# A layer-norm and weight-split step taken off GpSimd: one two-scalar VectorE operation for a chunk, all weight splits on VectorE

## The chip, the cores and the metric

The kernel runs on one core of a Trainium2 chip. The metric is the device time of one execution in microseconds (us). The engines are TensorE (PE), VectorE (DVE), ScalarE (ACT), GpSimd (POOL) and SyncE (SP), which only issues transfers here. Two times count as different when they are over 0.2% apart.

## The reference

Two layers of a block on 256 tokens of width 2048. Each layer projects its input, runs three mixers on the parts (a gated convolution, a gated linear recurrence, a retention), projects back, adds and normalizes, then does a feed-forward step of width 8192 and normalizes again. What touches the change is this:

```python
def layer_norm(x, g, b):
    xf = x.astype(jnp.float32)
    mu = jnp.mean(xf, axis=-1, keepdims=True)
    var = jnp.mean(jnp.square(xf - mu), axis=-1, keepdims=True)
    return (xf - mu) * lax.rsqrt(var + LN_EPS) * g + b

def reference(...):
...
    for l in range(DEPTH):
        proj = jnp.einsum('btd,de->bte', x, w_in[l])
...
        h = jnp.einsum('bte,ed->btd', mix, w_out[l])
        x = layer_norm(DEEPNORM_ALPHA * x + h, ln1_g[l], ln1_b[l]).astype(dtype)
        f = jnp.square(jax.nn.relu(jnp.einsum('btd,df->btf', x, w_ff1[l])))
        h = jnp.einsum('btf,fd->btd', f, w_ff2[l])
        x = layer_norm(DEEPNORM_ALPHA * x + h, ln2_g[l], ln2_b[l]).astype(dtype)
    return x
```

There are four such norms: two per layer.

## The kernel before, in words

**Weights in two parts.** All large products run as float32r matmuls of split numbers: a value is its rounded high part plus a low part. Weights come from memory in pieces of 1 MB into one of three `raw` buffers (`load2`, L268). A piece is two *units* of 128 x 1024. For each unit `unit()` lets ACT write the high part (L288) and then another engine the low part, raw minus high (L291), into one of six `wp` buffers. DVE does L291, except where `pool_lo` names the unit: there POOL does it.

**Products with the activation standing still.** `xstat` makes an output block of 512 columns for both halves of the tokens (`t` = 0 and 1, 128 tokens each) from eight units. `mmx` issues six matmuls (L313) per unit and half: for each of two row blocks high x high, high activation x low weight, low activation x high weight. With `tail` = 6 the last six units run all of t = 0 first, then all of t = 1, so that the norm of the first half can start early. With `head` = 6 the next product starts with units 1 to 6 of t = 0 before t = 1 comes in.

**The norm.** The class `Norm` runs at the end of such a product. For each half, the last of four chunks of 512 columns is added (L938 or L940), its statistics taken (L861), mean and variance combined (L872), epsilon added (L873). POOL raises the variance to the power -1/2 (L407), which gives the reciprocal deviation, and then multiplies mean and reciprocal, negated (L413, `nb`). DVE meanwhile takes chunks 0 to 2 minus mean times gain (L883), then times reciprocal plus bias (L889). Chunk 3 is *lazy*: its gain and bias are applied behind the transposition, so it needs only (x - mean) x reciprocal, which ACT does as scale and bias (L893) with the reciprocal and `nb`. PE transposes each chunk (L399, four 128 x 128 blocks); for chunk 3 ACT applies gain and bias (L913, four instructions); then ACT casts the high part (L388) and DVE makes the low part (L390), and the matmuls of the next product can use it. In the last norm of the kernel all four chunks go by L883 and L889 and then to memory, and `nb` is not read.

**The order.** Nothing is ordered by hand: `Plan.run` lists all operations with an engine, a cost, what they read and write, and picks for each engine, in simulated time, what can start earliest, by urgency. The order on each engine is then fixed, and the engines wait for each other by semaphores. An operation waits for its engine's earlier ones in any case. The norm's operations are given the highest urgency (`FIRST`, `NOW`), the low parts of weights are due when their matmuls are.

**Names.** `wp_64` to `wp_69` are the six `wp` buffers; at the first norm they hold units 1 to 6 of the next product. `act_72` to `act_75` hold the transposed activations that the norm makes, `act_76` to `act_79` the old ones, `aux_105` to `aux_108` the transposes in PSUM, `mm_101` to `mm_104` the sums. At the first norm `mm_102` is the last sum of t = 1 before the norm, `mm_103` the next product's for t = 0 and `mm_104` for t = 1. `sm_98` and `sm_99` hold the statistics of the two halves.

Of the kernel before, what the change touches and what calls it, by code (L numbers as in the profile page):

```python
# [14 lines left out]
AF = mybir.ActivationFunctionType  # L15
ALU = mybir.AluOpType
# [6 lines left out]
W = 512  # L23
# [17 lines left out]
WARM = 11  # L41
HEAD, TAIL = 6, 6

POOL_LO = (1, 3)


PACK = (("ident", P), ("tri", P), ("lbt", 12), ("hng", 12), ("rgg", 12), ("rgb", 12), ("clg", 8), ("clb", 8),
# [25 lines left out]
class Plan:  # L73
# [8 lines left out]
    def op(self, eng, cost, fn, r=(), w=(), slack=8.0, floor=8.0, need=None, after=(), chain=None, late=0.0, same=None):  # L82
        o = Op()
        o.eng, o.cost, o.fn, o.slack, o.floor, o.need, o.late = eng, cost, fn, slack, floor, need, late
        o.same = (0.0 if eng == "PE" else self.SAME) if same is None else same
        o.succ, o.ready, o.main, o.end = [], 0.0, None, None
        deps = {}
        bufs = []
        for items, wr in ((r, False), (w, True)):
            for it in items:  # L90
                b, part = it if isinstance(it, tuple) else (it, None)
                if b not in bufs:
                    bufs.append(b)
                keep = []
                for (p, pp, pw) in b.log:
                    hit = pp is None or part is None or pp == part
                    if hit and (wr or pw) and p is not o:
                        deps[p] = True
                        if wr and (part is None or pp == part):
                            continue  # L100
                    keep.append((p, pp, pw))
                keep.append((o, part, wr))
                b.log = keep
        for p in after:
            if p is not None:
                deps.setdefault(p, True)
        if chain is not None:
            p = self.last.get(chain)
            if p is not None:
                deps.setdefault(p, False)  # L110
            self.last[chain] = o
        for b in bufs:
            if b.ring is not None:
                b.uses += 1
        o.bufs = bufs
        o.deps = deps
        o.left = len(deps)
        for p, full in deps.items():
            p.succ.append((o, full))
        self.ops.append(o)  # L120
        return o
# [81 lines left out]
def block_kernel(ctx: ExitStack, tc: tile.TileContext, a: dict, out: bass.AP):  # L203
    nc = tc.nc
    V, S, G = nc.vector, nc.scalar, nc.gpsimd
# [3 lines left out]
    op = plan.op  # L209
# [14 lines left out]
    def keep(name, shape, dt=F32):  # L224
        return Buf(None, pool.tile(list(shape), dt, name=name))


    def act(n, ptr=0, ps=False):
        return 0.000833 * n + (0.051 if ps else 0.093) + 0.093 * ptr

    def dve(n, ptr=0, fast=False):
        return (0.00052 if fast else 0.001042) * n + 0.069 + 0.06 * ptr

    POOLC, POW = 0.26, 1.5
# [159 lines left out]
    def transpose4(src, r, **kw):  # L394
        pt = aux.buf()

        def fn():
            for i in range(4):
                nc.tensor.transpose(out=pt.t[:, i * P:(i + 1) * P], in_=src()[:, i * P:(i + 1) * P], identity=ident)  # L399

        op("PE", 0.44, fn, r=r, w=[pt], **kw)
        return pt

    def rsqrt(v, s, c0, n):

        y = s[:, c0:c0 + n]
        G.tensor_tensor(out=y, in0=v, in1=mhalf.t[:, 0:n], op=ALU.pow)  # L407
        return y

    def rsqrt1(s, mean, v):  # L410

        y = rsqrt(v, s, 37, 1)
        G.tensor_scalar(out=s[:, 48:49], in0=mean, scalar1=y, scalar2=-1.0, op0=ALU.mult, op1=ALU.mult)  # L413

    NOW, FIRST = dict(slack=-50.0, floor=-100.0), dict(slack=-200.0, floor=-300.0)

    mhalf = keep("mhalf", [P, 4])
# [416 lines left out]
    class Norm:  # L834
# [31 lines left out]
        def norm(self, t):  # L866
            if self.xT is None and not self.last:
                self.xT = [acts.buf() for _ in range(4)]
            s = self.s[t]
            mean, rstd, nb = (lambda: s.t[:, 24:25]), (lambda: s.t[:, 37:38]), (lambda: s.t[:, 48:49])  # L870
            def aggr():
                V.bn_aggr(out=s.t[:, 24:26], in_=s.t[:, 0:24])  # L872
                V.tensor_scalar(out=s.t[:, 26:27], in0=s.t[:, 25:26], scalar1=EPS, scalar2=None, op0=ALU.add)  # L873

            op("DVE", 0.2, aggr, w=[s], **FIRST)

            def rs():
                rsqrt1(s.t, mean(), s.t[:, 26:27])

            op("POOL", POW + POOLC, rs, r=[(s, "x"), mhalf], w=[(s, "r")], **FIRST)  # L880
            direct = range(4) if self.last else [c for c in range(4) if c not in LAZY]
            for c in direct:
                op("DVE", dve(W, 1), lambda c=c: V.scalar_tensor_tensor(  # L883
                    out=self.y(t, c), in0=self.y(t, c), scalar=mean(), in1=self.gb[c][0].t, op0=ALU.subtract,
                    op1=ALU.mult), r=[(s, "x"), self.gb[c][0]], w=[(x_nat, (t, c))], **NOW)
            for c in range(4):
                xk = (x_nat, (t, c))
                if c in direct:
                    op("DVE", dve(W, 1), lambda c=c: V.scalar_tensor_tensor(  # L889
                        out=self.y(t, c), in0=self.y(t, c), scalar=rstd(), in1=self.gb[c][1].t, op0=ALU.mult,  # L890
                        op1=ALU.add), r=[(s, "r"), self.gb[c][1]], w=[xk], **NOW)
                else:
                    op("ACT", act(W, 2), lambda c=c: S.activation(  # L893
                        out=self.y(t, c), in_=self.y(t, c), func=AF.Identity, scale=rstd(), bias=nb()),
                       r=[(s, "r")], w=[xk], **NOW)
                if self.last:
                    op("DMA", 0.8, lambda c=c: nc.sync.dma_start(
                        out=out[t * P:(t + 1) * P, c * W:(c + 1) * W], in_=self.y(t, c)), r=[xk], **NOW)
                    continue
                cols = slice(t * P, (t + 1) * P)  # L900
                if c not in LAZY:
                    if c not in direct:
                        self.affine(c, t, **NOW)
                    pt = transpose4(lambda c=c: self.y(t, c), [xk, cst], **NOW)
                    split_act(self.xT[c], slice(0, 4), cols, lambda pt=pt: pt.t, [pt], t, ps=True, **NOW)
                else:
                    pt = transpose4(lambda c=c: self.y(t, c), [xk, cst], **NOW)
                    z = r2.buf()

                    def fn(c=c, pt=pt, z=z):  # L910
                        for b in range(4):
                            k = 4 * c + b
                            S.activation(out=z.t[:, b * P:(b + 1) * P], in_=pt.t[:, b * P:(b + 1) * P],  # L913
                                         func=AF.Identity, scale=lng[:, self.n, k:k + 1], bias=lnb[:, self.n, k:k + 1])

                    op("ACT", 4 * act(P, 2, True), fn, r=[pt, cst], w=[z], **NOW)
                    split_act(self.xT[c], slice(0, 4), cols, lambda z=z: z.t, [z], t, **NOW)
# [28 lines left out]
    for l in range(DEPTH):  # L946
# [3 lines left out]
        def vgroup(g, **kw):  # L950
            tl = []
            vt.append(tl)

            def done(t, ps):
                v = r2.buf()
                op("ACT", act(W, ps=True), lambda: S.copy(out=v.t, in_=ps.t), r=[ps], w=[v], floor=1.5)
                tl.append(v)

            xstat(a["wv"][l, g], xT, done, **kw)
# [9 lines left out]
        else:  # L969
            vgroup(0, head=HEAD, pool_lo=POOL_LO)  # L970
            norm.rest()
        pairs, gates = {}, {}
        for i, (kind, p) in enumerate(ORDER):
# [11 lines left out]
            if l == 0 and i == 1:  # L985
                op("DMA", 6.0, lambda: nc.sync.dma_start(out=x_nat.t, in_=a["x"].rearrange("(t p) d -> p t d", p=P)),
                   w=[x_nat], after=(plan.last["PE"],))
            if kind == "hf":
                hgrn_gates(l, p, pr, pair)
            elif kind == "hq":  # L990
                Qv = pv(pair, 2)
                op("ACT", act(W), lambda Qv=Qv, pr=pr: S.activation(out=Qv(), in_=pr.t, func=AF.Sigmoid), r=[pr],
                   w=[(pair, "Q")])
                op("DVE", dve(W), lambda Qv=Qv, pr=pr: V.tensor_tensor(out=Qv(), in0=pr.t, in1=Qv(), op=ALU.mult),
                   r=[pr], w=[(pair, "Q")])
            elif kind == "hg":
                gate = r2.buf()
                op("ACT", act(W), lambda gate=gate, pr=pr: S.activation(out=gate.t, in_=pr.t, func=AF.Sigmoid),
                   r=[pr], w=[gate])
                hgrn(l, p, pairs["h", p], gate, vt, mixT)  # L1000
            elif kind in ("cg", "ca"):
# [4 lines left out]
                if kind == "cg":  # L1006
                    op("ACT", act(W), lambda uv=uv, pr=pr: S.activation(out=uv(), in_=bl(pr.t, 2), func=AF.Sigmoid),
                       r=[pr], w=uk)
                else:
                    op("DVE", dve(W), lambda uv=uv, pr=pr: V.tensor_tensor(out=uv(), in0=bl(pr.t, 2), in1=uv(),  # L1010
                                                                           op=ALU.mult), r=[pr], w=uk)
# [5 lines left out]
            elif kind == "rg":  # L1017
                gate = r2.buf()
                op("ACT", act(W), lambda gate=gate, pr=pr: S.activation(out=gate.t, in_=pr.t, func=AF.Sigmoid),
                   r=[pr], w=[gate])  # L1020
                op("DVE", dve(W), lambda gate=gate, pr=pr: V.tensor_tensor(out=gate.t, in0=pr.t, in1=gate.t,
                                                                           op=ALU.mult), r=[pr], w=[gate])
# [10 lines left out]
        for c in range(NCH):  # L1033
# [9 lines left out]
            if c == 0:  # L1043
                xstat(a["w1x"][l], xT, square_t, head=HEAD, pool_lo=POOL_LO)
                norm.rest()
            for q in range(2 if c == 0 else 0, 8):
                r = wstat(a["w1"][l, 8 * c + q - 2], xT)
                f = r2.buf()
                op("DVE", dve(W), lambda f=f, r=r: V.scalar_tensor_tensor(  # L1049
                    out=f.t, in0=r.t, scalar=0.0, in1=r.t, op0=ALU.max, op1=ALU.mult), r=[r], w=[f], floor=1.5)  # L1050
# [127 lines left out]
```

## Time and profile before

| what | value |
|---|---|
| median of 3 runs | 2340.0 us (2339.7 to 2341.8) |
| the profiled execution, its own time | 2341.02 us |
| its span, first to last instruction | 2339.2 us |
| mean granted TensorE clock | 0.998 |
| PE, DVE, ACT, POOL busy | 2320.4, 1504.0, 1054.0, 65.0 us |
| first norm's PE stretch, from the first transpose of t = 0 to the first matmul of t = 1 | 447.18 to 464.16 us |

The span is the profile's, from the first instruction to the last; the execution's own time is 1.8 us longer. PE's busy time is that of matmuls, which overlap; a wait of PE is read from the timeline, where the idle time ahead of an operation stands in brackets with what ended it. Lines are those of the kernel before.

### The profile page before, as it was taken

How to read it: one execution, taken by the hardware profiler on the slowest of the kernel's cores; microseconds unless marked ns; L12 is line 12 of the kernel's file. 1: busy time of each engine (PE TensorE's matmuls, PEld its weight loads, DVE VectorE, ACT ScalarE, POOL GpSimd, SP SyncE). 2: the span in 40 equal slices, each digit the busy share in tenths (PEclk: the TensorE clock that was granted, in tenths of full speed). 3: DMA queues.
4: the chain of work that ended last, by engine and by line, in shares of the span. 5: the costliest groups of instructions: out<-in, count | busy, mean ns of one | idle time of the engine just before them, and what ended most of it. 6: DMA issues, size and time to landing. Idle time of an engine off the chain costs nothing.

```text
span 2339.2 us, 29616 instructions
## 1 busy us (share of the span) xinstructions
PE 2320.4 (99%) x12067; PEld 1974.0 (84%) x12067; DVE 1504.0 (64%) x2046; ACT 1054.0 (45%) x1334; POOL 65.0 (3%) x66
## 2 busy tenths in 40 slices
PE   9999999999999999999999999999999999999998
PEld 7888888788888888888888888887888888888886
DVE  6997666665565565565579976656655655655655
ACT  6445444454344344344444455444543444443442
POOL 0000000100000000000000000101000000000000
PEclk9999999999999999999999999999999999999999
DMA  8544566465555555556454445564555555555563
GB/s 299 181 162 162 171 198 207 162 207 188 190 189 189 198 180 198 188 190 205 167 205 162 163 162 174 189 218 159 205 198 185 193 187 191 185 193 198 181 229 113
DMA packets 67705, 439.90 MB, mean 188 GB/s; under 512 B 7664, under 2 KB 7920, under 8 KB 16624
## 3 DMA queue, kind: packets, MB, share of 16 engines
q1 hardware_dynamic: 67568, 438.01, 55.0%
q8 instruction: 94, 1.54, 0.2%
q14 instruction: 43, 0.35, 0.0%
HBM read 432.74 MB, written 2.10 MB: 186 GB/s over the span
## 4 chain that ended last, share of the span: by engine, by line
PE 98%; DVE 1%; DMA 0%; ACT 0%; issue 0%; SPq 0%; DVEq 0%
PE mm L313 44%; PE mm L363 33%; PE mm L365 17%; PE aux L604 2%; PE aux L399 1%; DVE x_nat L889 0%; DMA raw<-in_wv 0%; PE aux L550 0%; PE aux L552 0%; PE aux L588 0%; PE aux L548 0%; PE aux L717 0%; DVE x_nat L883 0%; ACT r L913 0%; DVE sm L861 0%
## 5 line engine op out<-in xcount | busy, mean ns | idle before, releaser
L291 DVE TENSOR_TENSOR wp<-raw,wp 128x1024 fp32r<-128x1024 f32 (+1 forms) x796 | 970.9, 1221 | 602.4 <-ACT wp L288 600.6
L288 ACT CAST wp<-raw 128x1024 fp32r<-128x1024 f32 (+1 forms) x802 | 842.4, 1052 | 819.0 <-PE mm L313 561.7
L363 PE MATMUL mm<-act,wp 128*128 128x512 f32 x3328 | 1180.8, 399 | 0.0
L313 PE MATMUL mm<-wp,act 128*128 128x512 f32 x4608 | 1061.1, 390 | 3.9 <-ACT wp L288 1.7
L313 PEld LDWEIGHTS mm<-wp,act 128*128 128x128 f32 x4608 | 861.1, 188 | 185.4 <-ACT wp L288 2.9
L365 PE MATMUL mm<-act,wp 128*128 128x256 f32 x3328 | 933.2, 280 | 0.0
L363 PEld LDWEIGHTS mm<-act,wp 128*128 128x128 f32 x3328 | 625.4, 188 | 151.5
L365 PEld LDWEIGHTS mm<-act,wp 128*128 128x128 f32 x3328 | 628.4, 189 | 0.5
L372 ACT COPY r<-mm 128x256 f32<-128x256 f32 x208 | 77.9, 375 | 369.6 <-PE mm L365 369.3
L375 DVE TENSOR_TENSOR r<-mm,r 128x256 f32<-128x256 f32 x184 | 78.1, 424 | 146.2 <-ACT r L372 145.9
L791 DVE SCALAR_TENSOR_TENSOR r<-u_t,cst,r 128x256 f32<-128x256 f32 x240 | 102.1, 479 | 0.0
L407 POOL TENSOR_TENSOR sm<-sm,mhalf 128x4 f32<-128x4 f32 (+1 forms) x24 | 30.4, 1266 | 2252.5 <-DVE sm L873 1589.4
L388 ACT CAST act<-r 128x512 fp32r<-128x512 f32 x82 | 51.5, 628 | 21.7 <-DVE r L1049 16.2
L390 DVE TENSOR_TENSOR act<-r,act 128x512 fp32r<-128x512 f32 x82 | 57.9, 706 | 0.0
L604 PEld LDWEIGHTS aux<-pair 128*128 128x128 f32 x336 | 42.4, 191 | 2.6
L1049 DVE SCALAR_TENSOR_TENSOR r<-r 128x512 f32<-128x512 f32 x60 | 41.6, 693 | 2.1
L604 PE MATMUL aux<-pair 128*128 128x64 f32 x336 | 42.0, 267 | 0.0
L940 DVE TENSOR_TENSOR x_nat<-x_nat,mm 128x512 f32<-128x512 f32 x48 | 30.8, 681 | 12.7 <-PE mm L313 12.7
L938 DVE SCALAR_TENSOR_TENSOR x_nat<-x_nat,mm 128x512 f32<-128x512 f32 x32 | 20.6, 680 | 11.7 <-PE mm L313 11.7
L889 DVE SCALAR_TENSOR_TENSOR x_nat<-x_nat,sm,r 128x512 f32<-128x512 f32 x26 | 24.3, 989 | 0.0
L609 DVE COPY_PREDICATED r<-maskl,aux 128x256 f32<-128x256 uint8 x42 | 21.9, 521 | 0.0
L375 DVE TENSOR_TENSOR pair<-mm,r 128x256 f32<-128x256 f32 x24 | 10.2, 423 | 17.8 <-ACT r L372 17.8
(115 smaller groups left out, 513.4 us busy)
## 6 DMA issues: line engine op xcount, KB each, us to landing
raw<-in_w SPq DMA_DIRECT2D x248, 1024.0 KB, 4.8
raw<-in_wp SPq DMA_DIRECT2D x88, 1024.0 KB, 4.8
raw<-in_wo SPq DMA_DIRECT2D x32, 1024.0 KB, 4.8
raw<-in_wv SPq DMA_DIRECT2D x20, 1024.0 KB, 4.8
raw<-in_w1x SPq DMA_DIRECT2D x8, 1024.0 KB, 4.8
raw<-in_wv SPq DMA_DIRECT2D x6, 512.0 KB, 6.0
pair<-pair SPq DMA_DIRECT2D x24, 128.0 KB, 2.3
x_nat<-in_x SPq DMA_DIRECT2D x1, 2048.0 KB, 9.4
```

The source lines that it names most:

```text
L288: S.copy(out=u.w.t[:, 0, sl], in_=raw.t[:, rs])
L291: (G if pool_lo else V).tensor_tensor(out=u.w.t[:, 1, sl], in0=raw.t[:, rs], in1=u.w.t[:, 0, sl].bitcast(F32), op=ALU.subtract)
L313: nc.tensor.matmul(ps.t, lhsT=xT[k // 4].t[:, xs, k % 4, t * P:(t + 1) * P], rhs=w[:, ws, kb, :], start=(k == 0 and n == 0), stop=(k == KB ...
L363: nc.tensor.matmul(pv, lhsT=w[:, 0, kb, :], rhs=xt[:, :, k % 4, :], start=(k == 0), stop=False)
L365: nc.tensor.matmul(pv[:, 0, :], lhsT=w[:, 1, kb, :], rhs=xt[:, 0, k % 4, :], start=False, stop=(k == KB - 1))
L372: S.copy(out=low.t, in_=ps.t[:, T:])
L375: V.tensor_tensor(out=dst[2]()[:, b * T:(b + 1) * T], in0=ps.t[:, 0:T], in1=low.t, op=ALU.add)
L388: op("ACT", act(n, ps=ps), lambda: S.copy(out=x.t[:, 0, blks, cols], in_=bl(src(), nb)), r=r, w=[(x, part)], **kw)
L390: op("DVE", dve(n), lambda: V.tensor_tensor(out=x.t[:, 1, blks, cols], in0=bl(src(), nb), in1=x.t[:, 0, blks, cols].bitcast(F32), op=ALU.s ...
L604: nc.tensor.matmul(ps.t[:, b * 64:(b + 1) * 64], lhsT=Kt()[:, b * P:(b + 1) * P], rhs=rhs, start=True, stop=True)
L791: V.scalar_tensor_tensor(out=d, in0=src, scalar=cw[:, l, b, j:j + 1], in1=d, op0=ALU.mult, op1=ALU.add)
L1049: op("DVE", dve(W), lambda f=f, r=r: V.scalar_tensor_tensor(out=f.t, in0=r.t, scalar=0.0, in1=r.t, op0=ALU.max, op1=ALU.mult), r=[r], w=[f ...
```

## The change

No unit is left to POOL: `POOL_LO` is empty, so the units 2 and 4 of three products (the two first products on `w1x`, and the first of the second layer on `wv`), six in all, are split by DVE. In `Norm.norm` POOL does only the power; the product of mean and reciprocal goes, in all four norms. Chunk 3 is normalized by one DVE operation that subtracts the mean and multiplies by the reciprocal, both of them columns of the statistics tile; for the three norms with two halves these are six instructions, which ACT had before. Its planned cost changes with it.

```diff
-POOL_LO = (1, 3)
+POOL_LO = ()
...
-            mean, rstd, nb = (lambda: s.t[:, 24:25]), (lambda: s.t[:, 37:38]), (lambda: s.t[:, 48:49])
+            mean, rstd = (lambda: s.t[:, 24:25]), (lambda: s.t[:, 37:38])
...
-            def rs():
-                rsqrt1(s.t, mean(), s.t[:, 26:27])
-
-            op("POOL", POW + POOLC, rs, r=[(s, "x"), mhalf], w=[(s, "r")], **FIRST)
+            op("POOL", POW, lambda: rsqrt(s.t[:, 26:27], s.t, 37, 1), r=[(s, "x"), mhalf], w=[(s, "r")], **FIRST)
...
-                    op("ACT", act(W, 2), lambda c=c: S.activation(
-                        out=self.y(t, c), in_=self.y(t, c), func=AF.Identity, scale=rstd(), bias=nb()),
-                       r=[(s, "r")], w=[xk], **NOW)
+                    op("DVE", dve(W, 2, True), lambda c=c: V.tensor_scalar(
+                        out=self.y(t, c), in0=self.y(t, c), scalar1=mean(), scalar2=rstd(), op0=ALU.subtract,
+                        op1=ALU.mult), r=[(s, "x"), (s, "r")], w=[xk], **NOW)
```

The planner puts the operations around the three norms in another order. Lines of the changed kernel behind the edit are three lower: L935 is L938, L880 is L883, L886 is L889, and the new operation is L890.

VectorE before, at the first norm, from the last addition of t = 1 on (`act_75` is chunk 3 of t = 0):

```order
L938 SCALAR_TENSOR_TENSOR x_nat<-x_nat,mm_102 128x512
L390 TENSOR_TENSOR act_75<-r_6_86,act_75 128x4x128
L861 BN_STATS sm_99<-x_nat 128x6
L291 TENSOR_TENSOR wp_68<-raw_62,wp_68 128x1024
L872 BN_AGGR sm_99<-sm_99 128x2
L873 TENSOR_SCALAR sm_99<-sm_99 128x1
L291 TENSOR_TENSOR wp_69<-raw_62,wp_69 128x1024
L883 SCALAR_TENSOR_TENSOR x_nat<-x_nat,sm_99,r_8_88 128x512
...
L889 SCALAR_TENSOR_TENSOR x_nat<-x_nat,sm_99,r_10_90 128x512
...
L390 TENSOR_TENSOR act_72<-aux_107,act_72 128x4x128
```

VectorE in the changed kernel, from the same addition on (`act_74` is now chunk 3 of t = 0):

```order
L935 SCALAR_TENSOR_TENSOR x_nat<-x_nat,mm_102 128x512
L390 TENSOR_TENSOR act_74<-r_6_86,act_74 128x4x128
L861 BN_STATS sm_99<-x_nat 128x6
L390 TENSOR_TENSOR act_75<-aux_106,act_75 128x4x128
...
L291 TENSOR_TENSOR wp_66<-raw_61,wp_66 128x1024
L880 SCALAR_TENSOR_TENSOR x_nat<-x_nat,sm_99,r_8_88 128x512
...
L890 TENSOR_SCALAR x_nat<-x_nat,sm_99 128x512
L886 SCALAR_TENSOR_TENSOR x_nat<-x_nat,sm_99,r_10_90 128x512
...
L291 TENSOR_TENSOR wp_67<-raw_61,wp_67 128x1024
L390 TENSOR_TENSOR act_72<-aux_108,act_72 128x4x128
...
L291 TENSOR_TENSOR wp_68<-raw_62,wp_68 128x1024
L291 TENSOR_TENSOR wp_69<-raw_62,wp_69 128x1024
```

The splits of `wp_66` to `wp_69` moved: before, all that DVE had of them came ahead of the three L883; now only `wp_66` does, `wp_67` follows the three L889 (L886), and `wp_68` and `wp_69` follow the four L390 of t = 1.

TensorE before, at the first norm, from the first matmuls of the next product on:

```order
L313 MATMUL mm_103<-wp_64,act_72 128x512 x6
...
L313 MATMUL mm_103<-wp_68,act_74 128x512 x6
L313 MATMUL mm_103<-wp_69,act_74 128x512 x6
L399 MATMUL aux_108<-cst,x_nat 128x128 x4
L399 MATMUL aux_107<-cst,x_nat 128x128 x4
L399 MATMUL aux_105<-cst,x_nat 128x128 x4
L399 MATMUL aux_106<-cst,x_nat 128x128 x4
L313 MATMUL mm_104<-wp_64,act_72 128x512 x6
```

TensorE in the changed kernel, from the same matmuls on:

```order
L313 MATMUL mm_103<-wp_64,act_72 128x512 x6
L313 MATMUL mm_103<-wp_65,act_72 128x512 x6
L313 MATMUL mm_103<-wp_66,act_73 128x512 x6
L399 MATMUL aux_107<-cst,x_nat 128x128 x4
L399 MATMUL aux_108<-cst,x_nat 128x128 x4
L399 MATMUL aux_105<-cst,x_nat 128x128 x4
L399 MATMUL aux_106<-cst,x_nat 128x128 x4
L313 MATMUL mm_103<-wp_67,act_73 128x512 x6
L313 MATMUL mm_103<-wp_68,act_75 128x512 x6
L313 MATMUL mm_103<-wp_69,act_75 128x512 x6
L313 MATMUL mm_104<-wp_64,act_72 128x512 x6
```

The sixteen transposes of t = 1, chunk 3 (`aux_107`) first, moved ahead of the matmuls on units 4 to 6. Of the sixteen transposes of t = 0, the last four moved behind six matmuls of `mm_102`.

## Rows read from the trace of the kernel before

**Rows 1.** The page, part 1: busy us (share of the span) xinstructions.
```profile
PE 2320.4 (99%) x12067; PEld 1974.0 (84%) x12067; DVE 1504.0 (64%) x2046; ACT 1054.0 (45%) x1334; POOL 65.0 (3%) x66
```

**Rows 2.** The page, part 4: the chain that ended last, by engine.
```profile
PE 98%; DVE 1%; DMA 0%; ACT 0%; issue 0%; SPq 0%; DVEq 0%
```

**Rows 3.** Timeline of PE at the first norm: start us, us, operation [idle before <-releaser].
```profile
447.18 1.03 PE L399 MATMUL aux<-cst,x_nat 128*128 128x128 f32 x8
449.41 1.32 PE L399 MATMUL aux<-cst,x_nat 128*128 128x128 f32 x8 [1.19 <-DVE x_nat L889]
450.48 11.16 PE L313 MATMUL mm<-wp,act 128*128 128x512 f32 x48
461.49 2.28 PE L399 MATMUL aux<-cst,x_nat 128*128 128x128 f32 x16
464.16 11.42 PE L313 MATMUL mm<-wp,act 128*128 128x512 f32 x48 [0.40 <-ACT act L388]
```

**Rows 4.** Timeline of PE, the same place at the second and third norms.
```profile
1165.87 1.32 PE L399 MATMUL aux<-cst,x_nat 128*128 128x128 f32 x8 [1.11 <-DVE x_nat L889]
...
1611.79 1.32 PE L399 MATMUL aux<-cst,x_nat 128*128 128x128 f32 x8 [1.18 <-DVE x_nat L889]
```

**Rows 5.** Timeline of DVE at the first norm; the second row is from a narrower stretch.
```profile
445.82 4.20 DVE L889 SCALAR_TENSOR_TENSOR x_nat<-x_nat,sm,r 128x512 f32<-128x512 f32 x3
446.48 2.88 DVE L889 SCALAR_TENSOR_TENSOR x_nat<-x_nat,sm,r 128x512 f32<-128x512 f32 x1
...
449.94 1.21 DVE L291 TENSOR_TENSOR wp<-raw,wp 128x1024 fp32r<-128x1024 f32 x1
451.08 0.68 DVE L390 TENSOR_TENSOR act<-aux,act 128x512 fp32r<-128x512 f32 x1
...
454.01 0.67 DVE L938 SCALAR_TENSOR_TENSOR x_nat<-x_nat,mm 128x512 f32<-128x512 f32 x1
454.60 1.25 DVE L390 TENSOR_TENSOR act<-r,act 128x512 fp32r<-128x512 f32 x1
...
457.51 0.25 DVE L872 BATCH_NORM_AGGREGATE sm<-sm 128x2 f32<-128x24 f32 x1
...
457.86 1.22 DVE L291 TENSOR_TENSOR wp<-raw,wp 128x1024 fp32r<-128x1024 f32 x1
459.00 2.07 DVE L883 SCALAR_TENSOR_TENSOR x_nat<-x_nat,sm,r 128x512 f32<-128x512 f32 x3
460.99 2.07 DVE L889 SCALAR_TENSOR_TENSOR x_nat<-x_nat,sm,r 128x512 f32<-128x512 f32 x3
```

**Rows 6.** Timeline of POOL at the first norm.
```profile
444.06 0.95 POOL L407 TENSOR_TENSOR sm<-sm,mhalf 128x1 f32<-128x1 f32 x1 [87.55 <-DVE sm L873]
...
445.91 2.90 POOL L291 TENSOR_TENSOR wp<-raw,wp 128x1024 fp32r<-128x1024 f32 x1
452.90 2.41 POOL L291 TENSOR_TENSOR wp<-raw,wp 128x1024 fp32r<-128x1024 f32 x1 [4.09 <-ACT wp L288]
458.02 1.47 POOL L407 TENSOR_TENSOR sm<-sm,mhalf 128x1 f32<-128x1 f32 x1 [2.71 <-DVE sm L873]
```

**Rows 7.** The chain in order of time: start us, us, what (four transposes).
```profile
475.59 0.44 PE aux L399 x4
```

**Rows 8.** Groups by line and shape: xcount | busy us, mean ns | idle before.
```profile
L791 DVE SCALAR_TENSOR_TENSOR r<-u_t,cst,r 128x256 f32<-128x256 f32 x240 | 102.1, 479 | 0.0
...
L788 DVE TENSOR_SCALAR r<-u_t,cst 128x256 f32<-128x256 f32 x8 | 2.9, 411 | 0.2
```

**Rows 9.** Timeline of ACT at the first norm, second half.
```profile
462.12 1.51 ACT L913 ACTIVATE r<-aux,cst 128x128 f32<-128x128 f32 x4 [0.82 <-PE aux L399]
463.51 1.58 ACT L388 CAST act<-aux 128x512 fp32r<-128x512 f32 x3
```

**Rows 10.** Stretches: length, busy us of PE, PEld, DVE, ACT, POOL; PEclk, DMA share, GB/s.
```profile
12.80:14.40 1.60, 0.00 (x0) 0.00 (x0) 0.00 (x0) 1.01 (x1) 0.00 (x0) 1.00 0.97 341
2329.10:2331.10 2.00, 0.00 (x0) 0.00 (x0) 1.90 (x5) 0.00 (x0) 0.07 (x1) 1.00 0.31 123
2331.10:2333.10 2.00, 0.00 (x0) 0.00 (x0) 2.00 (x4) 0.00 (x0) 1.78 (x2) 0.57 0.01 4
```

**Rows 11.** The page, part 6: loads of raw, us to landing.
```profile
raw<-in_w SPq DMA_DIRECT2D x248, 1024.0 KB, 4.8
```

## The prediction

> **What bounds the kernel now.** I read the busy times first [rows 1]: TensorE (PE) is busy for 2320.4 of 2339.2 us, VectorE (DVE) for 64% of the span, ScalarE (ACT) for 45%, GpSimd (POOL) for 3%. The chain of waits says the same [rows 2]: 98% of it is PE. So only what moves PE's few idle microseconds can move the time, and the work that the change touches is used at three places, the first three layer norms (the fourth norm reads the same helper but ends the kernel). The next view is the timeline of PE at the first norm [rows 3]. PE does eight transposes from 447.18, then idles 1.19 us for L889, does eight more, runs 48 matmuls from 450.48, sixteen transposes from 461.49 and goes on at 464.16. The same gap of 1.11 and 1.18 us stands at the other two norms [rows 4], so I work one norm out and take it three times.
>
> The timeline of DVE shows what the first gap is [rows 5]. Three L889 from 445.82 take 4.20 us; the second alone takes 2.88 where its equals take about 0.74 (three in 2.07 at 460.99). POOL's timeline [rows 6] has its weight split from 445.91, 2.90 us long, and the slow L889 ends 0.55 us after that split does. At 452.90 POOL splits again, and the L390 of 454.60, which reads two tiles in SBUF, takes 1.25 in place of 0.68, while the L390 at 451.08 and the L938 at 454.01, each with one input in PSUM, keep 0.68 and 0.67. The other way round, the power of 458.02 takes 1.47 where that of 444.06 took 0.95, with a DVE split from 457.86 to 459.08. So DVE and POOL wait for each other when both read SBUF, and that is the gap which the change can close.
> The Trainium skill states this as a rule (SBUF — State Buffer, "Who interferes with whom"): the two share a port pair, a DVE operation with two SBUF inputs and a GpSimd operation that reads SBUF exclude each other, and the later one blocks until the first is done. The trace agrees (2.88 for about 0.74 us). By that rule alone DVE gets back all of the stall, which is the faster rival's gain below.
>
> **The change, part by part.** Steps are start to start: two neighbours on DVE overlap by 0.08 us (L938 lasts 0.67 and the next starts after 0.59 [rows 5]). I take 0.60 for the half-wide steps (L938, L390, L861), 1.14 for a split L291 of 1.22, 1.99 for three L883 or three L889 (459.00 to 460.99), 0.35 for L872 with L873. On PE a matmul of L313 costs 0.227 and a restart 0.1 (48 take 11.01 from 450.48 to 461.49 [rows 3]), four transposes cost 0.44 [rows 7].
>
> *Product of mean and deviation.* Six POOL operations (and two in the last norm) go. Each stood between the power and the ACT operation L893. In the last norm nothing waits for it: DVE has four L883 to do meanwhile. Nothing is gained there.
>
> *The normalized chunk.* Six ACT operations L893 become six DVE operations with two scalars. That form exists at half the width: L788, 0.411 us for 256 columns, less than the 0.479 of L791 [rows 8]. At 512 columns it is at least 0.41 (no growth) and at most 0.82 (twice). I take 0.54: L791 has one scalar, too, and grows by 0.26 from 256 columns to the 0.74 of L889 at 512, so its fixed part is about 0.21. With that L788's 256 columns cost at most 0.20; a second scalar makes the fixed part larger and the columns cheaper, and I put them at half of 0.26, 0.13. Start to start that is 0.47. ACT's relief is worth nothing, as ACT has 55% idle.
>
> *The weight splits.* Six of POOL's L291 (2.4 to 2.9 us each) become DVE's at 1.14. On DVE a norm thus gains 2 x 1.14 + 2 x 0.47 = 3.2 us of work and loses 2.13 + 0.57 = 2.7 us of stall. The sum hardly moves; what moves is the order. POOL had units 2 and 4 (wp_65, wp_67), and DVE did units 3, 5 and 6 (wp_66, wp_68, wp_69) ahead of the second half's normalization. Now unit 3 stands right before the three L883, unit 4 behind the three L889, units 5 and 6 behind the four L390, and PE's second transposes stand ahead of units 4 to 6. PE runs the first matmul of a unit with the high part alone; the second reads what L291 writes.
>
> *First half.* DVE: L889 445.82, the new operation 446.48, two L889 from 446.95, splits and L390 from 448.27 to 451.75, no stall. PE: three chunks from 447.18 to 448.50, six matmuls to 449.96, one chunk to 450.40, six matmuls to 451.86; each chunk is there in time. The last result is there at 452.05, where before it was at about 453.5 (450.48 + 0.1 + 12 x 0.227 + 0.19). **Gain 1.45 us.**
>
> *Second half, DVE.* It starts at 452.05 with L938 and from there never rests: L390, L861, L390 to 454.45; L872 and L873 to 454.80; split wp_66, ended 456.02; three L883 from 455.94; the new operation from 457.93, ended 458.47; three L889, ended 459.14, 459.80, 460.47; split wp_67 from 460.39, ended 461.61; four L390 from 461.53; split wp_68 from 463.93, ended 465.15; split wp_69, ended 466.29. The power lies under the split wp_66 and the L883. The four L390 need ACT's casts: L913 starts some 0.2 us after the transposes, the casts follow 1.39 us later [rows 9], so from 460.6 on, one each 0.48, which is 0.3 us or more ahead of DVE.
>
> *Second half, PE.* Twelve matmuls on wp_64 and wp_65 to 454.58, one on wp_66 to 454.81. Wait for wp_66 until 456.08: 1.27. Five matmuls (1.24) to 457.32. Wait for the new operation until 458.53: 1.21. Four chunks at DVE's pace of 0.66 to 460.97: 0.68 lost. One matmul on wp_67 to 461.30, wait until 461.67: 0.37. Five to 462.91, one to 463.14, wait for wp_68 until 465.21: 2.07. Five to 466.45, six on wp_69 to 467.81. There the matmuls of the second half (mm_104) begin. Before they began at 464.16, and those 48 lost 0.26 more than the 48 of 450.48, which hold one restart: 464.52 without. **Per norm 467.81 - 464.52 = 3.3 us lost**, the 1.45 gained at first already in it.
>
> Behind that nothing is late: the weights for the next units need PE's release of the same buffers, which comes after mm_104's matmuls, and the raw buffers (freed at 461.6 and 466.3) are reloaded in 4.8 us [rows 11] before that. Nor is anything caught up, since PE has no idle time there.
>
> **Sum:** 3 x 3.3 = +9.9 us. On the profiled execution, 2341.02, that is 2350.9; it stands 1.0 above the median of 2340.0, so a median of **2350**. With the new operation at 0.41 each norm loses 0.13 less, at 0.82 0.28 more (-0.4 and +0.8 in all); a wait misread by 0.7 us per norm is 2 us.
>
> **The rivals.**
> *Faster:* the closed gap decides. If PE keeps the 1.45 us of the first half and the second half loses no more than now, the time is 2340 - 4.35 = 2335.6. For it speaks the stall of 2.13 us that surely goes. Against it: the split of wp_66 would have to end before 454.8 and that of wp_68 before 463.1, so DVE's chain from 452.05 would have to be 1.2 to 2.1 us shorter, while its operations cost as much where POOL rests. 7%.
> *No change:* the waits for wp_66 and wp_68 come out at half, so that gain and loss cancel within 0.2%, about 2342. It needs a DVE chain 1.7 us shorter per norm, some 13%; nothing in the rows gives that. 7%.
> *Slower still, by the clock:* the granted clock stayed 1.00 from 12.8 to 14.4 with no matmul at all, yet was 0.57 on average in 2331.1 to 2333.1, after PE's last matmul ended at 2329.0 [rows 10]. PE will idle four times in 11 us, 2.07 at the longest. If the clock fell to its lower level for the next 12 matmuls, each would cost 0.227 more: 2.7 us per norm, 2358. Against it: from 2329.1 to 2331.1 PE idled as long as it will here, and the clock was still 1.00. 6%.
> The Trainium skill (TensorE: Matmul & The Clock Gate, "HAM oscillation — how this bites in real kernels") says that waits between bursts of matmuls can throw the engine back to the low clock again and again; here no such thing is seen at gaps of 1.2 us.
>
> **How the numbers follow.** The forecast has 80%. Its own range is 2346 to 2354 (the bounds of the new operation, the misread wait, the spread of runs). To hold 8 in 10 I reach a little into both neighbours: 2344 to 2355. A measurement here tells 0.2%, 4.7 us, from no change. Slower by more: the forecast and the clock, 86%; within: 8%, the no-change case and the forecast's edge; faster: 6%.
>
> **What would show it.** Right: no POOL split, L889 at 0.74 everywhere, no gap near 448; PE idle behind L291 (twice, about 1.3 and 2.1 us) and behind the new operation (1.2) at each of three norms, some 3.3 us more per norm from the first transposes to mm_104; the new operation near 0.54. Wrong: PE reaching mm_104 near 463, a new operation of 0.8, or idle time outside the norms.

## The result, and the profile after

The changed kernel took 2351.22 us (median of 5 runs, 2350.35 to 2353.37), the kernel before 2341.64 beside it: a ratio of 1.0044, 95% interval [1.0034, 1.0055]. It is slower, by some 10 us. The profiled execution took 2351.37, with a span of 2349.6.

The page of the changed kernel, parts 1 and 4, for [rows 1, 2]:

```profile
PE 2323.7 (99%) x12067; PEld 1975.5 (84%) x12067; DVE 1505.5 (64%) x2058; ACT 1048.6 (45%) x1328; POOL 41.3 (2%) x52
...
PE 97%; DVE 2%; DMA 1%; issue 0%; ACT 0%; SPq 0%; DVEq 0%; ACTq 0%
```

POOL lost 24 us of work, and DVE gained only 1.5: what it got in splits and normalized chunks, it saved in stalls. Of the ten microseconds PE's busy time took 3.3 and its idle time the rest. Where that idle time lies shows in the groups by line (count, busy us and mean ns, idle before and its releasers):

```profile
L313 PE MATMUL mm<-wp,act 128*128 128x512 f32 x4608 | 1065.1, 391 | 11.3 <-DVE wp L291 10.8 <-ACT wp L288 0.4
L399 PE MATMUL aux<-cst,x_nat 128*128 128x128 f32 x96 | 15.0, 300 | 3.1 <-DVE x_nat L890 3.1
```

In the kernel before, the first of these groups had this:

```profile
L313 PE MATMUL mm<-wp,act 128*128 128x512 f32 x4608 | 1061.1, 390 | 3.9 <-ACT wp L288 1.7 <-ACT act L388 1.2 <-DVE wp L291 1.0
```

The matmuls of L313 wait 10.8 us for DVE's splits (9.0 of them at the three norms), which was 1.0 us in the kernel before, and the transposes wait for the new operation in place of a slow L889. The timeline of PE at the first norm, for [rows 3]:

```profile
446.33 1.47 PE L399 MATMUL aux<-cst,x_nat 128*128 128x128 f32 x12
447.56 1.64 PE L313 MATMUL mm<-wp,act 128*128 128x512 f32 x6
449.03 0.60 PE L399 MATMUL aux<-cst,x_nat 128*128 128x128 f32 x4
449.39 4.59 PE L313 MATMUL mm<-wp,act 128*128 128x512 f32 x19
455.09 1.43 PE L313 MATMUL mm<-wp,act 128*128 128x512 f32 x5 [1.12 <-DVE wp L291]
457.54 2.64 PE L399 MATMUL aux<-cst,x_nat 128*128 128x128 f32 x16 [1.02 <-DVE x_nat L890]
459.93 0.48 PE L313 MATMUL mm<-wp,act 128*128 128x512 f32 x1
460.66 1.66 PE L313 MATMUL mm<-wp,act 128*128 128x512 f32 x6 [0.24 <-DVE wp L291]
464.19 15.30 PE L313 MATMUL mm<-wp,act 128*128 128x512 f32 x59 [1.87 <-DVE wp L291]
```

The gap between the first transposes is gone, and four others stand in the second half. The same rows at the third norm, the first transposes and from the last wait on:

```profile
1616.74 1.47 PE L399 MATMUL aux<-cst,x_nat 128*128 128x128 f32 x12
...
1634.61 13.70 PE L313 MATMUL mm<-wp,act 128*128 128x512 f32 x59 [1.88 <-DVE wp L291]
```

From the first transpose to the end of the last wait it takes 17.86 us at the first norm and 17.87 at the third: the same waits. But the 59 matmuls behind them take 15.30 us at the first and 13.70 at the third. The stretches around the first (columns as in [rows 10]) tell why:

```profile
460.00:464.20 4.20, 2.09 (x10) 1.16 (x8) 4.20 (x7) 1.71 (x4) 0.00 (x0) 1.00 0.63 201
464.20:466.20 2.00, 2.00 (x8) 1.64 (x9) 1.07 (x1) 0.00 (x0) 0.00 (x0) 0.87 0.26 107
466.20:469.00 2.80, 2.80 (x8) 2.20 (x7) 0.00 (x0) 0.00 (x0) 0.00 (x0) 0.50 0.94 313
469.00:475.00 6.00, 6.00 (x27) 4.90 (x26) 3.64 (x3) 3.16 (x3) 0.00 (x0) 0.99 0.23 53
```

The granted clock was at its lower level (0.50, that is 1.2 of 2.4 GHz) soon after PE had taken up work again, and 1.6 us were lost by it. At the third norm it stayed at 1.00. At the second it fell, too, but earlier, at the sixteen transposes behind waits of 1.12 and 1.01 us (rows of PE, then a stretch):

```profile
1178.87 3.52 PE L399 MATMUL aux<-cst,x_nat 128*128 128x128 f32 x16 [1.01 <-DVE x_nat L890]
...
1185.56 6.64 PE L313 MATMUL mm<-wp,act 128*128 128x512 f32 x28 [1.45 <-DVE wp L291]
```

```profile
1179.00:1181.50 2.50, 2.50 (x13) 2.40 (x14) 2.50 (x4) 1.63 (x5) 0.00 (x0) 0.52 0.00 0
```

These transposes took 3.52 us where the first norm's took 2.64, but PE then waited less for DVE's split, and the last wait ended 17.89 us behind the first transpose, as at the other norms: nothing was lost by it there.

The timeline of DVE in the same place, for [rows 5], and that of POOL, for [rows 6]:

```profile
444.95 0.75 DVE L886 SCALAR_TENSOR_TENSOR x_nat<-x_nat,sm,r 128x512 f32<-128x512 f32 x1
445.62 0.54 DVE L890 TENSOR_SCALAR x_nat<-x_nat,sm 128x512 f32<-128x512 f32 x1
446.07 1.41 DVE L886 SCALAR_TENSOR_TENSOR x_nat<-x_nat,sm,r 128x512 f32<-128x512 f32 x2
...
453.82 1.21 DVE L291 TENSOR_TENSOR wp<-raw,wp 128x1024 fp32r<-128x1024 f32 x1
454.95 2.07 DVE L880 SCALAR_TENSOR_TENSOR x_nat<-x_nat,sm,r 128x512 f32<-128x512 f32 x3
456.94 0.54 DVE L890 TENSOR_SCALAR x_nat<-x_nat,sm 128x512 f32<-128x512 f32 x1
457.40 2.07 DVE L886 SCALAR_TENSOR_TENSOR x_nat<-x_nat,sm,r 128x512 f32<-128x512 f32 x3
459.38 1.22 DVE L291 TENSOR_TENSOR wp<-raw,wp 128x1024 fp32r<-128x1024 f32 x1
...
462.91 2.36 DVE L291 TENSOR_TENSOR wp<-raw,wp 128x1024 fp32r<-128x1024 f32 x2
```

```profile
443.20 0.94 POOL L407 TENSOR_TENSOR sm<-sm,mhalf 128x1 f32<-128x1 f32 x1 [87.42 <-DVE sm L873]
454.05 1.40 POOL L407 TENSOR_TENSOR sm<-sm,mhalf 128x1 f32<-128x1 f32 x1 [9.90 <-DVE sm L873]
```

No operation of DVE is stalled any more (0.75 for each L886), and the new one takes 0.54. From 451 on DVE runs without a pause, with the splits for which PE waits behind the normalization.

### The profile page after: what moved, and what is told of

Its sections match the earlier page's. It is cut to its first block, busy times and chain, and to the rows that moved or that the text cites. A ratio compares the mean times of both kernels' runs of the same rounds, so it can differ in the third digit from the quotient of the medians.

```text
span 2349.6 us, 29609 instructions
## 1 busy us (share of the span) xinstructions
PE 2323.7 (99%) x12067; PEld 1975.5 (84%) x12067; DVE 1505.5 (64%) x2058; ACT 1048.6 (45%) x1328; POOL 41.3 (2%) x52
## 4 chain that ended last, share of the span: by engine, by line
PE 97%; DVE 2%; DMA 1%; issue 0%; ACT 0%; SPq 0%; DVEq 0%; ACTq 0%
PE mm L313 43%; PE mm L363 33%; PE mm L365 17%; PE aux L604 1%; PE aux L399 1%; DMA raw<-in_xt 1%; DVE wp L291 0%; DVE act L390 0%; DVE x_nat L880 0%; DVE x_nat L886 0%; PE aux L550 0%; PE aux L552 0%; PE aux L588 0%; PE aux L548 0%; DMA raw<-in_wv 0%; PE aux L717 0%
## 5 line engine op out<-in xcount | busy, mean ns | idle before, releaser
L313 PE MATMUL mm<-wp,act 128*128 128x512 f32 x4608 | 1065.1, 391 | 11.3 <-DVE wp L291 10.8
L313 PEld LDWEIGHTS mm<-wp,act 128*128 128x128 f32 x4608 | 861.3, 188 | 194.7 <-DVE wp L291 15.5
L390 DVE TENSOR_TENSOR act<-r,act 128x512 fp32r<-128x512 f32 x82 | 56.2, 685 | 0.0
L935 DVE SCALAR_TENSOR_TENSOR x_nat<-x_nat,mm 128x512 f32<-128x512 f32 x32 | 20.6, 682 | 11.9 <-PE mm L313 11.7
L375 DVE TENSOR_TENSOR pair<-mm,r 128x256 f32<-128x256 f32 x24 | 10.2, 424 | 17.8 <-ACT r L372 17.8
L623 DVE TENSOR_TENSOR pair<-pair 128x256 f32<-128x256 f32 (+1 forms) x42 | 17.0, 406 | 6.9 <-PE aux L604 6.7
```

The lines of the kernel that those rows point to most:

```text
L313: nc.tensor.matmul(ps.t, lhsT=xT[k // 4].t[:, xs, k % 4, t * P:(t + 1) * P], rhs=w[:, ws, kb, :], start=(k == 0 and n == 0), stop=(k == KB ...
L375: V.tensor_tensor(out=dst[2]()[:, b * T:(b + 1) * T], in0=ps.t[:, 0:T], in1=low.t, op=ALU.add)
L390: op("DVE", dve(n), lambda: V.tensor_tensor(out=x.t[:, 1, blks, cols], in0=bl(src(), nb), in1=x.t[:, 0, blks, cols].bitcast(F32), op=ALU.s ...
```

## The experiments

The theory: DVE does hardly more work than before, and it is the **order** into which the planner puts it that costs 3.3 us per norm. The rivals: the **amount** of DVE's work, one of the **two parts** of the change alone, and the **clock**. Times are medians; each is compared with the kernel before on the same chip (2340.92, then 2341.08, then 2341.16), so ratios are what may be compared between them. Many of the differences below are under the 0.2% that counts here; those I take from the interval of the ratio together with PE's rows.

### One part at a time

The splits alone, on the kernel before:

```diff
-POOL_LO = (1, 3)
+POOL_LO = ()
```

> Only the weight splits go to VectorE; chunk 3 stays on ScalarE and GpSimd keeps the product. Theory (what counts is where VectorE's splits stand against the norm of the second half): the planner now puts the splits of units 3 and 4 ahead of the three L883 and those of units 5 and 6 behind the L889 and behind the four L390, so PE waits once, about 2 us, for unit 6; worked out as before, mm_104 begins near 466.4 in place of 464.5, +1.9 us per norm, so about 5.8 us over the kernel before (2346 to 2348). Rival A (the new VectorE operation costs the time): no more than 1 us over before. Rival B (the splits alone cost it, by their amount): all of the 9.6 us.

Measured: 2348.47 (2346.65 to 2352.57), ratio 1.0031 [1.0020, 1.0043]. Some 7 us slower, a little over what was expected. From the first transposes to the transposes that follow the norm (`r`, L399) PE takes 30.06 us at the first norm (447.40 to 477.46), and took 28.24 before (447.18 to 475.42): 1.8 us a norm, as expected. The rest is the clock, which fell at the second norm of this profile (0.50 from 1186 to 1188) and at neither of the others. The timeline of PE at the first norm:

```profile
458.89 2.41 PE L399 MATMUL aux<-cst,x_nat 128*128 128x128 f32 x16 [0.79 <-ACT x_nat L893]
461.06 0.48 PE L313 MATMUL mm<-wp,act 128*128 128x512 f32 x1
461.78 1.67 PE L313 MATMUL mm<-wp,act 128*128 128x512 f32 x6 [0.24 <-DVE wp L291]
465.31 5.06 PE L313 MATMUL mm<-wp,act 128*128 128x512 f32 x21 [1.86 <-DVE wp L291]
```

With chunk 3 still on ACT the same wait of 1.9 us for a split stands there: it comes with the splits.

The chunk (and the product) alone, on the changed kernel:

```diff
-POOL_LO = ()
+POOL_LO = (1, 3)
```

> Only chunk 3 goes to VectorE and the product goes; GpSimd keeps its six splits. Theory: GpSimd's split of unit 2 now begins before the new operation and holds it and the L889 behind it by 2 us or more, so PE's gap at the first transposes stays or grows, and unit 6's split stands behind the L889: 3 to 8 us over the kernel before. Rival A (the new operation costs the time): about 9 us over before with GpSimd's stalls no worse than before. Rival B (the splits alone cost it): within 2 us of before.

Measured: 2353.66 (2350.43 to 2354.12), ratio 1.0047 [1.0035, 1.0060], well over the expected. The timelines of PE, DVE and POOL at the first norm:

```profile
448.81 0.66 PE L399 MATMUL aux<-cst,x_nat 128*128 128x128 f32 x4 [1.44 <-DVE x_nat L886]
451.30 1.32 PE L399 MATMUL aux<-cst,x_nat 128*128 128x128 f32 x8 [1.83 <-DVE x_nat L890]
452.37 2.46 PE L313 MATMUL mm<-wp,act 128*128 128x512 f32 x6
```

```profile
445.84 2.92 DVE L886 SCALAR_TENSOR_TENSOR x_nat<-x_nat,sm,r 128x512 f32<-128x512 f32 x1
448.67 2.57 DVE L890 TENSOR_SCALAR x_nat<-x_nat,sm 128x512 f32<-128x512 f32 x1
```

```profile
445.82 2.38 POOL L291 TENSOR_TENSOR wp<-raw,wp 128x1024 fp32r<-128x1024 f32 x1 [0.80 <-ACT wp L288]
448.52 2.43 POOL L291 TENSOR_TENSOR wp<-raw,wp 128x1024 fp32r<-128x1024 f32 x1 [0.32 <-ACT wp L288]
```

POOL's two splits now stand next to each other, and each blocks an operation of DVE: L886 for 2.2 us and the new one for 2.0 (2.57 for 0.54). PE waits for both, 3.3 us, where before it waited 1.19 here; the six matmuls behind take 2.46 where 1.64 is their time, as the clock had fallen (0.50 from 453.0 to 455.5), which it did at all three norms of this profile. I had expected one operation to be blocked, not two, and no loss by the clock.
The Trainium skill (SBUF — State Buffer, "Who interferes with whom") says that a `tensor_scalar` may use both of DVE's ports, and then excludes GpSimd as two inputs do. The trace agrees: this one has a single tensor for its input, and was blocked (2.57 us for 0.54).

So neither part is a gain by itself as the planner places it, and the two costs (7 and 11 us) don't add up to the 10 of both: with the splits gone from POOL, the chunk has nothing to be blocked by. From the splits alone to the whole change the ratio rises from 1.0031 to 1.0044, 3 us, while two operations of 0.47 us start to start at three norms make 2.8. That pair doesn't price the chunk alone, though: with the splits alone the planner puts two of them ahead of the three L883, and in the changed kernel one.

### The order alone

The changed kernel, with the same instructions, and the splits of units 3 to 6 given so high an urgency that they come ahead of the second half's norm (the last number of an operation says by how many us it counts as due ahead of its matmuls):

```diff
-POOL_LO = ()
+POOL_LO, EARLY = (), (2, 3, 4, 5)
...
-                      (op(eng, cost, lo, r=[rk], w=[(u.w, pt)], chain="lo" + eng), 1.3)]
+                      (op(eng, cost, lo, r=[rk], w=[(u.w, pt)], chain="lo" + eng), 300.0 if early else 1.3)]
...
-                us[i] = unit(ld, i % 2, i in pool_lo)
+                us[i] = unit(ld, i % 2, i in pool_lo, head > 0 and i in EARLY)
```

> The changed kernel with the same instructions on every engine, but the low parts of units 3 to 6 get an urgency above the norm's, so that VectorE does them ahead of the last addition of the second half; PE's second transposes then stand behind all six units again. Theory (order): PE no longer waits for a split; it waits about 2 us for the low part of the second chunk, and mm_104 begins near 464.9, so the time is within 2 us of the kernel before, 7 to 9 us under the changed kernel. Rival (amount of VectorE work, in whatever order): the same as the changed kernel, 9 to 10 us over before.

Measured: 2344.77 (2342.04 to 2347.7), ratio 1.0014 [1.0005, 1.0023]. The same on the kernel before, with its splits on DVE and chunk 3 left to ACT:

> All splits on VectorE in the order with units 3 to 6 ahead of the norm, chunk 3 on ScalarE as before. Theory (order): VectorE has 0.47 us less per half in the norm than in the run with the new operation, mm_104 begins near 464.6, within 1.5 us of the kernel before and at most 1 us under the run with the new operation. Rival (the amount of VectorE work): 5 us over before.

Measured: 2344.22 (2341.84 to 2345.33), ratio 1.0012 [1.0003, 1.0020]. In both, some two thirds of the loss are back, from the order alone (of the 10 us, and of the 7 of the splits alone), and the rival by amount falls. Both end 1.3 to 1.9 us above the most that was expected. PE in the first of them:

```profile
457.21 5.29 PE L313 MATMUL mm<-wp,act 128*128 128x512 f32 x22 [1.98 <-DVE act L390]
462.34 2.11 PE L399 MATMUL aux<-cst,x_nat 128*128 128x128 f32 x16
465.01 11.45 PE L313 MATMUL mm<-wp,act 128*128 128x512 f32 x48 [0.56 <-ACT act L388]
```

One wait of 1.98 us is left, for the L390 that now stands behind five splits in a row, beside 0.56 for a cast, where the kernel before had 0.40. The clock fell at the third norm of this profile alone (the same 22 matmuls took 6.90 us there), and at all three with chunk 3 on ACT.

A milder urgency spreads the splits among the steps of the second half. On the changed kernel (`54 if early`), and on the kernel before with its splits on DVE and chunk 3 on ACT (`54` and `56`):

> The changed kernel with the same instructions, and the four splits of units 3 to 6 put among the steps of the second half instead of behind its normalization: DVE does wp_66 before the second L938, wp_67 to wp_69 around the statistics, then the second normalization; PE does all six units' matmuls ahead of the second transposes. Order theory: the waits of PE become four of at most 1 us per norm (about .15, .4, .95, .35) and the second half's matmuls start where they do in the kernel before within .3 us: 2340 to 2343, 8 to 11 us under the changed kernel. If the clock is what the first such order lost in addition (its one wait was 1.98 us), this one, without a wait near 2 us, shows no stretch at the lower clock at the norms and is 1.5 to 4 us faster than it. Rival (the amount of DVE work decides, whatever its order): no more than 6 us under the changed kernel.

> The kernel before with the two GpSimd splits given to DVE, chunk 3 left on ScalarE, and the same placing of the splits among the second half's steps. Order theory: PE's waits are .2 to .65 us each, the second half's matmuls start about .9 us earlier per norm than in the kernel before: 2337 to 2339.5. Rival (GpSimd's help with the splits is worth its stall): slower than before, 2343 or more.

> As the one with chunk 3 on ScalarE, the splits a place earlier still: one wait of .95 us and no other, the second half's matmuls start about .95 us earlier per norm than in the kernel before: 2337 to 2339.5, the same as its neighbour within 1 us. If it comes out over 2343, the place of single splits decides more than I hold.

Measured: **2341.68** (2340.09 to 2342.05), ratio 1.0002 [0.9993, 1.0010] for the changed kernel in this order; **2338.66** (2337.12 to 2340.72), 0.9989 [0.9981, 0.9998], and **2338.39** (2337.37 to 2340.12), 0.9988 [0.9979, 0.9996], with chunk 3 on ACT. All three came as expected. PE at the first norm, in the first and in the last of them:

```profile
449.54 10.57 PE L313 MATMUL mm<-wp,act 128*128 128x512 f32 x42
460.90 2.64 PE L399 MATMUL aux<-cst,x_nat 128*128 128x128 f32 x16 [0.79 <-DVE x_nat L890]
463.62 11.49 PE L313 MATMUL mm<-wp,act 128*128 128x512 f32 x48
```

```profile
459.82 0.66 PE L399 MATMUL aux<-cst,x_nat 128*128 128x128 f32 x4 [0.82 <-ACT x_nat L893]
...
463.32 11.53 PE L313 MATMUL mm<-wp,act 128*128 128x512 f32 x48
```

No wait is over 0.82 us, and the clock was 1.00 at all three norms of each. The whole loss of the change is undone with its own instructions, by the urgency of four splits alone. The pair of 54 also gives the price of the chunk (with the product that goes with it): 2341.68 against 2338.66 is 3.0 us for its place on DVE. The pair with the splits first shows only 0.5 us (2344.77 and 2344.22), but there the clock fell at more norms of the one with ACT's chunk; with the waits filled, below, that pair stands at ratios of 1.0010 and 0.9999, 2.6 us apart. The two with chunk 3 on ACT and no split on POOL end below both kernels, by some 2.5 us below the kernel before: 0.8 per norm of the 1.19 us gap. That is 0.1%, clear of the interval but under the 0.2% that counts as a difference here; PE's rows agree with it, with 463.32 less 447.31, 16.01 us from the first transpose to the second half's matmuls, for 16.98 before.

### The clock

To see what the clock takes, the waits were filled with matmuls whose results are overwritten, so that they add work and compute nothing. In the run with the splits first (2344.77), eight of them in the wait of 1.98 us:

```diff
+                        if fill is not None and kb == kbs[0] and n == 1:
+                            for _ in range(8):
+                                nc.tensor.matmul(fill.t, lhsT=wz.t[:, 0:P], rhs=wz.t, start=True, stop=True)
...
-            mmx(us[i], ps[t], xT, i, t)
+            mmx(us[i], ps[t], xT, i, t, ps[1] if head and (i, t) == (2, 0) else None)
```

> The changed kernel with the early splits (the run of 2344.8), and eight matmuls of 512 columns more in each of the three norms, put into PE's one wait of 1.98 us there; their results are overwritten, so they add work and no value. Clock theory (what that run lost over the kernel before is the granted clock falling behind the wait): no stretch at half clock at the norms, 1 to 2.5 us under that run, near 2342.5. Rival (the wait itself is all, and the clock costs nothing): the same time within .5 us; and if the eight matmuls delay the split's reader, slower by up to 1 us.

Measured: 2343.06 (2342.25 to 2345.52), ratio 1.0010 [1.0001, 1.0019]; no low stretch at a norm. That is 1.7 us less by the medians and 0.9 by the ratios, whose intervals overlap, so this run alone doesn't decide. In the same way in the run with the splits first and ACT's chunk (2344.22, the lower clock at all three norms), nine of them, and in the changed kernel itself five in the wait for `wp_66` and eight in that for `wp_68`:

> The kernel before with its GpSimd splits on DVE and all splits done first (the run of 2344.2, whose profile shows the lower clock at all three norms), with nine matmuls of 512 columns more in the one wait of 2.21 us; their results are overwritten, so they add work and no value. Clock theory: no low stretch, 1 to 2.5 us under that run, 2341.7 to 2343.2. Rival: the same within .5 us, since the wait itself stays.

> The changed kernel with matmuls of 512 columns added in two of its waits at each of the three norms, five in the wait for wp_66 and eight in the wait for wp_68; their results are overwritten, so they add work and no value. Order theory with the clock as a small part: no stretch of the lower clock at the norms any more, and the order's own loss stays, so 0.5 to 2 us under the changed kernel's 2351.2 (in its profile one low stretch cost 1.6 us, the other lay in a wait): 2349 to 2350.7. Rival (the lower clock is a good part of the loss): 2347 or less. Rival (it costs nothing): 2351.2 within .5.

Measured: 2341.30 (2339.29 to 2342.47), ratio 0.9999 [0.9991, 1.0008], a little better than expected; and 2352.14 (2350.17 to 2353.02), ratio 1.0043 [1.0030, 1.0057], no better than the changed kernel without them, a miss. The rows of PE at the first norm, from the filled wait on, first the run with ACT's chunk without filling, then with it (the trace has eight of the nine), then the filled changed kernel; lines behind the added ones are three higher, so L402 is L399 and L393 is L390:

```profile
456.58 5.54 PE L313 MATMUL mm<-wp,act 128*128 128x512 f32 x16 [2.21 <-DVE act L390]
```

```profile
456.21 1.89 PE L318 MATMUL mm<-wz 128*128 128x512 bf16 x8
458.35 3.97 PE L313 MATMUL mm<-wp,act 128*128 128x512 f32 x16 [0.25 <-DVE act L393]
```

```profile
449.39 1.47 PE L402 MATMUL aux<-cst,x_nat 128*128 128x128 f32 x12
...
465.18 1.90 PE L318 MATMUL mm<-wz 128*128 128x512 bf16 x8
467.24 13.71 PE L313 MATMUL mm<-wp,act 128*128 128x512 f32 x59 [0.16 <-DVE wp L291]
```

Sixteen matmuls take 3.97 us in place of 5.54, and the 59 behind the last wait of the changed kernel 13.71 in place of 15.30, so filling keeps the clock up and is worth 1.6 us where it had fallen. The wait itself stays: from the first transpose 449.39 to 467.24 it is 17.85 us, as in the changed kernel's 17.86. Why the filled changed kernel shows nothing of it in the median is open in part: its profiled execution came to the first norm 3.06 us later than the other (449.39 against 446.33), with a granted clock of 0.72 from 10 to 22 us, at the program's start, where the other profile has 1.00; and with five runs of each the interval is wider than 1.6 us. That the clock is a *part* of the loss is supported by three pairs of profiles that point the same way, by PE's stretch from the first transpose to its last matmul: with the splits first it went from 4.3 us over the kernel before to 2.4, with ACT's chunk from 3.8 to 0.2, in the changed kernel from 11.2 to 9.8. And in the five kernels with a wait of 1.8 us or more at a norm the clock fell at 10 of 15 norms, in the three filled ones at none of 9. How large it is in the median of the changed kernel isn't settled, beyond at most 1.6 us for a norm in which it falls.

## Why the prediction was right

It said 2350, in 2344 to 2355, slower: 2351.2 was measured. Point by point, at the first norm:

- **The stall goes.** Right: L889 (now L886) takes 0.75 everywhere, and no gap stands near 448. What its end is worth alone no run shows; the two kernels in a better order, which end 0.8 us a norm under the kernel before, have it in their sum. Of the two operations that I read as spared by POOL's splits, with one input in PSUM, one shows nothing: POOL has no operation at 451.08 [rows 6], so the L390 there had nothing to wait for. The L938 of 454.01, beside a POOL split, does show it.
- **The new operation, 0.54.** Measured 0.54, at all six places.
- **The product, ACT's relief, POOL: nothing.** Nothing in PE's waits hangs on them.
- **First half.** The last addition of t = 1 (L935) was to start at 452.05; it started at 451.06 in a trace that is 0.85 us ahead there (446.33 for 447.18), which makes 451.91. Right within 0.15.
- **Second half.** The waits were to be 1.27, 1.21, 0.37 and 2.07; the profile has 1.12, 1.02, 0.24 and 1.87, each for the operation that I named. Each is 0.13 to 0.20 smaller, since the profile counts a wait from the modelled end of the matmul before (a single one has a row of 0.48), and I from 0.227 behind its start; from the first transposes to the end of the last wait I had 18.03 (465.21 less 447.18), and 17.86 was measured. So the order costs 3.1 us per norm rather than 3.3, 9.4 in all.
- **Nothing behind it is late.** Right: what PE lost at the norms it kept, and no wait was added elsewhere.
- **The clock.** Here I was wrong in part. I gave it 6%, since the clock had not fallen in 2 us of idle time at the end of the trace [rows 10]. It fell at two of three norms of this profile. The price was 1.6 us rather than 2.7, at one norm only, since at the second it lay inside a wait. So the sum is 9.4 and 1.6, less 0.85 that the profiled run was ahead at the first norm: 10.2, where its own time is 10.35 us longer (2351.37 against 2341.02). The step that failed is the reading of [rows 10]: it took the clock inside a gap for the clock behind it. Here, too, the clock was 1.00 while PE waited (460.00 to 464.20) and fell behind the wait, and [rows 10] have 0.57 from 2331.1 on, with no matmul left to pay for it. That the number was hit so closely is luck in part, as the smaller waits made room for the clock.
 The Trainium skill (TensorE: Matmul & The Clock Gate, "HAM oscillation — how this bites in real kernels") had it that waits between bursts throw the engine back to the low clock; the trace agrees now at the first norm, with 1.02, 0.24 and 1.87 us of waits ahead of the 0.50, but not at the third, with the same waits and 1.00.
- **DVE's work barely grows, the order decides.** Shown, by the same instructions in another order at 2341.68. But there is a part that the order doesn't touch: the chunk on DVE costs 2.6 to 3.0 us in the two pairs in which the clock stayed at 1.00 at the norms. I put it down to DVE being what PE waits for from the last addition to the last transposes; the sum of 2.8 above fits that.

## What to carry to other kernels

When an engine on the critical path for 20 us gets more work, ask of each operation who waits for it, and then whether the scheduler will put it ahead of or behind those that are waited for: here the same instructions made 2351 or 2342 us. Taking GpSimd off a shared resource was worth some 2.5 us (0.1%) once the splits were placed by a set urgency and the chunk stayed on an engine that was idle; see which engine is idle before you give a step to the one that the others wait for. Waits between matmuls can cost more than their sum, by the clock.

## What the runs showed of the hardware that I had not expected

- The granted clock fell to 0.50 behind waits of 1 to 2.2 us, in some norms and not in others that had the same waits (1.87 at the first norm of the changed kernel, where it fell; 1.88 at the third, where it didn't). One wait alone can do it: 2.21 us with the splits first and ACT's chunk, at all three norms. Where no wait was over 1.19 us (the kernel before and the three orders with short waits), and in the three runs with filled ones, it fell at no norm.
- Matmuls without a purpose can be worth their time: nine in a wait of 2.2 us took the 16 matmuls behind from 5.54 to 3.97 us.
- An operation of DVE with one tensor and two scalars is blocked by a GpSimd split as one with two tensors is: 2.57 us for 0.54.
